# Channel shuffle: loads and stores in turn on one queue, with half tiles at both ends

## The chip, the cores and the metric

The kernel runs on one core of a Trainium2 chip. The core has several engines with instruction streams of their own: TensorE (PE), VectorE (DVE), ScalarE (ACT), GpSimd (POOL) and SyncE (SP). Data moves between the main memory (HBM) and the on-chip memory of 128 partitions by 16 DMA engines, which work from queues; a transfer is put on a queue by an instruction on one of the engine streams, here SyncE or ScalarE. In the profile "SPq" and "ACTq" are those issuing streams, and "q1" and "q10" their DMA queues.

The metric is the device time of one execution in microseconds, the median of several runs. Beside it there is one profiled execution with a trace.

## The reference

The input `x` has the shape 16 x 64 x 64 x 256, float32, 67.11 MB. The 256 channels are seen as 8 groups of 32, and the two are swapped:

```python
x = x.reshape(batch, h, w, groups, channels_per_group)
x = x.transpose(0, 1, 2, 4, 3)
x = x.reshape(batch, h, w, c)
```

Each of the 65,536 rows of 256 numbers is thus permuted within itself: channel g·32 + j goes to j·8 + g. No arithmetic is done. All 67.11 MB must be read and all 67.11 MB written.

## The kernel before

The 65,536 rows are cut into 8 tiles of 64 rows a partition (`_SLOTS = [[64]] * 8`). A tile is 128 partitions x 64 rows x 256 numbers, 64 KB a partition and 8.39 MB in all, contiguous in main memory. On chip it lives in a slot; three slots (`_BUFS = 3`) are used in rotation, each with room for 68 rows a partition.

Every tile goes through three steps.

1. Load (line 55): one transfer, issued by SyncE, puts the tile into its slot four rows after the slot's beginning (`_SHIFT = 4`).
2. Permute (line 64): 16 copies on VectorE, each of 4 rows a partition (1,024 numbers). A copy reads 4 rows and writes them, permuted, 4 rows earlier in the same slot. It writes where the copy before it has read, so no second buffer is needed, and the copies of a tile follow each other in order.
3. Store (line 68): one transfer, issued by ScalarE, of the 64 permuted rows that now stand at the beginning of the slot.

The order on each engine is the order in which the program is written (`manual_schedule`). Only the data and the slots make an engine wait: a copy waits for the tile's load, a store for the tile's 16 copies, and a load for the store of the tile that had the slot three tiles earlier. So loads 0, 1 and 2 are issued at once, and load k+3 waits on SyncE until store k has landed. Loads are on one queue and stores on another, and both queues may have work at the same time.

Of the kernel before, what the change touches and what calls it, by code (L numbers as in the profile page):

```python
# [1 line left out]

# [4 lines left out]


F32 = mybir.dt.float32
P = 128  # L10


_SLOTS = [[64]] * 8
_BUFS = 3

_SHIFT = 4


@with_exitstack
def kernel(  # L20
    ctx: ExitStack,
    tc: tile.TileContext,
    x: bass.AP,
    groups: bass.AP,
    out: bass.AP,
):
    nc = tc.nc
    b, h, w, c = x.shape
    G = int(groups)
    CPG = c // G  # L30
    assert G * CPG == c
    assert sum(map(sum, _SLOTS)) * P == b * h * w
    room = max(map(sum, _SLOTS)) + _SHIFT

    x_flat = x.rearrange("b h w c -> (b h w c)")
    out_flat = out.rearrange("b h w c -> (b h w c)")

    pool = ctx.enter_context(tc.tile_pool(name="pool", bufs=_BUFS))

    def rows(flat, first, q):  # L40

        return flat[first * c : (first + P * q) * c].rearrange("(p f) -> p f", p=P)

    ctx.enter_context(tc.manual_schedule(engines=None))
    first = 0
    for parts in _SLOTS:
        slot = pool.tile([P, room * c], F32, name="slot")
        at = 0
        pieces = []
        for q in parts:  # L50
            pieces.append((q, first, at))
            first += P * q
            at += q
        for q, start, at in pieces:
            nc.sync.dma_start(  # L55
                out=slot[:, (at + _SHIFT) * c : (at + _SHIFT + q) * c],
                in_=rows(x_flat, start, q),
            )
        for q, start, at in pieces:
            for lo in range(at, at + q, _SHIFT):  # L60
                n = min(_SHIFT, at + q - lo)
                src = slot[:, (lo + _SHIFT) * c : (lo + _SHIFT + n) * c]
                dst = slot[:, lo * c : (lo + n) * c]
                nc.vector.tensor_copy(  # L64
                    out=dst.rearrange("p (i j g) -> p i j g", j=CPG, g=G),
                    in_=src.rearrange("p (i g j) -> p i j g", g=G, j=CPG),
                )
            nc.scalar.dma_start(
                out=rows(out_flat, start, q), in_=slot[:, at * c : (at + q) * c]
            )  # L70


# [1 line left out]
_INS = ['x', 'groups']  # L74
_OUTS = [((16, 64, 64, 256), 'float32')]

_NUMBERS = {'groups': 8}


# [26 lines left out]
```

## Time and profile before

| | us |
|---|---|
| median of 3 runs | 322.84 (321.92 to 322.93) |
| the profiled execution | 322.83 |
| its span, first to last instruction | 321.1 |
| VectorE busy, 128 copies | 140.2 |
| a copy, mean | 1.095 |
| VectorE idle before a copy, for a load | 155.2, in 8 waits |
| SyncE waiting on line 55 for stores to land | 233.9, in 5 waits |
| issue to landing, loads (least, median, most) | 21.9, 44.1, 77.4 |
| issue to landing, stores (least, median, most) | 20.7, 55.7, 61.2 |

The profile counts the time that an engine spends in its instructions as busy; issuing a transfer is not counted. A transfer is listed with its issue and its landing. The DMA share is the mean busy share of the 16 DMA engines, and the GB/s are what they moved, reads of main memory and writes to it together. "Idle before, releaser" says what an instruction was waiting for when its engine stood still. In the chain of waits, each step is followed back to what released it. Some of its steps for this kernel are marked as released from "another core or an unknown queue"; they lie in the middle of the span, between one load's issue and the next.

### The profile page before, as it was taken

Reading aid. Unit: us, or ns where it says so; the run is one execution under the profiler, and the core shown is the slowest. Engines: PE = TensorE matmul, PEld = TensorE weight load, DVE = VectorE, ACT = ScalarE, POOL = GpSimd, SP = SyncE. Lnnn points to the kernel's source line nnn. Section 1 sums busy time; section 2 is a strip of 40 time slices with the busy share of each in tenths; the row PEclk is TensorE's granted clock in tenths of the full one; section 3 lists DMA queues with packets and bytes.
Section 4 is the critical chain, followed back from the end, with each engine's and each line's share of the span. In section 5 each row is a group of like instructions: output and inputs, shape, how many; then the busy total and the mean of one; then the engine's idle time right before and its main releaser. Section 6 shows DMA issues by size and latency. Waiting matters only on the chain.

```text
span 321.1 us, 207 instructions
## 1 busy us (share of the span) xinstructions
DVE 140.2 (44%) x128; POOL 0.2 (0%) x4
## 2 busy tenths in 40 slices
DVE  0019989401990006950069500795007940099300
POOL 0000000000000000000000000000000000000000
DMA  9999999999999999999999999999999999994696
GB/s 392 392 400 514 392 392 392 523 392 392 514 400 392 506 408 392 450 457 392 449 457 400 425 465 416 425 465 400 408 498 384 416 482 408 416 482 188 261 523 261
DMA packets 2305, 134.23 MB, mean 418 GB/s; under 512 B 256, under 2 KB 256, under 8 KB 256
## 3 DMA queue, kind: packets, MB, share of 16 engines
q1 hardware_dynamic: 1152, 67.11, 49.0%
q10 hardware_dynamic: 1152, 67.11, 48.3%
q14 instruction: 1, 0.01, 0.0%
HBM read 67.11 MB, written 67.11 MB: 418 GB/s over the span
## 4 chain that ended last, share of the span: by engine, by line
another core or an unknown queue 48%; DMA 33%; DVE 11%; SPq 0%; issue 0%; DVEq 0%
DMA slot<-in_x_dram 20%; DMA out_dram<-slot 13%; DVE slot L64 11%; SPq L55 0%; DVEq L64 0%
## 5 line engine op out<-in xcount | busy, mean ns | idle before, releaser
L64 DVE COPY slot<-slot 128x1024 f32<-128x1024 f32 x128 | 140.2, 1095 | 159.3 <-DMA slot<-in_x_dram 155.2
L87 POOL MEMSET const-bfloat16-1.0<- 128x1 bf16 x1 | 0.1, 101 | 0.0
L87 POOL MEMSET const-uint8-127<- 128x1 uint8 x1 | 0.1, 101 | 0.0
L87 POOL MEMSET const-float32-0.0<- 128x1 f32 x1 | 0.1, 98 | 0.2 <-issue 0.2
L87 POOL MEMSET const-float32-1.0<- 128x1 f32 x1 | 0.1, 98 | 0.0
## 6 DMA issues: line engine op xcount, KB each, us to landing
slot<-in_x_dram SPq DMA_DIRECT2D x8, 44.1
out_dram<-slot ACTq DMA_DIRECT2D x8, 55.7
```

The costliest lines, as they stand in the source:

```text
L64: nc.vector.tensor_copy(out=dst.rearrange("p (i j g) -> p i j g", j=CPG, g=G), in_=src.rearrange("p (i g j) -> p i j g", g=G, j=CPG),)
L87: nc = _bacc.Bacc("TRN2", target_bir_lowering=False, num_devices=1)
```

## The change

The slots stay three and of the same size. What changes:

- The tiles are nine: one of 32 rows a partition, seven of 64, one of 32 (`_TILES`). The first and the last are half as large, 4.19 MB and 8 copies each. The two half tiles move in transfers of 32 KB a partition.
- Stores are issued by SyncE, on the same queue as the loads. ScalarE issues nothing.
- The program is written so that SyncE's order is load 0, load 1, store 0, load 2, store 1, load 3, and so on to load 8, store 7, store 8: store k, and then load k+2.

The waits by data and by slots remain as they were. Load k+2 takes the slot of tile k-1, so it waits for the landing of store k-1; load 2 takes the third slot, which is free. On SyncE, what stands behind a waiting instruction waits with it: load k+2 cannot be issued before store k, and store k not before the copies of tile k. The copies themselves and their order on VectorE are the same, 128 in all.

```diff
-_SLOTS = [[64]] * 8
+_TILES = [32] + [64] * 7 + [32]
+_AHEAD = 2
 _BUFS = 3
...
+    queue = nc.sync
...
+    def load(k):
+        q = _TILES[k]
+        slots[k] = pool.tile([P, room * c], F32, name="slot")
+        queue.dma_start(
+            out=slots[k][:, _SHIFT * c : (_SHIFT + q) * c], in_=rows(x_flat, firsts[k], q)
+        )
+
+    def permute(k):
+        q, slot = _TILES[k], slots[k]
+        for lo in range(0, q, _SHIFT):
...
+            nc.vector.tensor_copy(
+                out=dst.rearrange("p (i j g) -> p i j g", j=CPG, g=G),
+                in_=src.rearrange("p (i g j) -> p i j g", g=G, j=CPG),
+            )
+
+    def store(k):
+        q = _TILES[k]
+        queue.dma_start(out=rows(out_flat, firsts[k], q), in_=slots.pop(k)[:, : q * c])
+
     ctx.enter_context(tc.manual_schedule(engines=None))
-    first = 0
-    for parts in _SLOTS:
...
-            nc.sync.dma_start(
...
-            nc.scalar.dma_start(
-                out=rows(out_flat, start, q), in_=slot[:, at * c : (at + q) * c]
-            )
+    n = len(_TILES)
+    for k in range(-_AHEAD, n):
+        if k >= 0:
+            permute(k)
+            store(k)
+        if k + _AHEAD < n:
+            load(k + _AHEAD)
```

More of the change, by code (lines that the diff above doesn't have):

```diff
@@ L31 @@
     assert G * CPG == c
-    assert sum(map(sum, _SLOTS)) * P == b * h * w
-    room = max(map(sum, _SLOTS)) + _SHIFT
+    assert sum(_TILES) * P == b * h * w
+    room = max(_TILES) + _SHIFT
     x_flat = x.rearrange("b h w c -> (b h w c)")
@@ L38 @@
     pool = ctx.enter_context(tc.tile_pool(name="pool", bufs=_BUFS))
+    queue = nc.sync
     def rows(flat, first, q):
         return flat[first * c : (first + P * q) * c].rearrange("(p f) -> p f", p=P)
-    ctx.enter_context(tc.manual_schedule(engines=None))
-    first = 0
-    for parts in _SLOTS:
[L47 to L54, printed above, removed]
-            nc.sync.dma_start(
-                out=slot[:, (at + _SHIFT) * c : (at + _SHIFT + q) * c],
-                in_=rows(x_flat, start, q),
-            )
[L59 to L68, printed above, removed]
-                out=rows(out_flat, start, q), in_=slot[:, at * c : (at + q) * c]
-            )
@@ new lines @@
+    firsts = [P * sum(_TILES[:k]) for k in range(len(_TILES))]
+    slots = {}
+    def load(k):
[7 more added lines that the diff above has]
+        for lo in range(0, q, _SHIFT):
+            n = min(_SHIFT, q - lo)
+            src = slot[:, (lo + _SHIFT) * c : (lo + _SHIFT + n) * c]
+            dst = slot[:, lo * c : (lo + n) * c]
+            nc.vector.tensor_copy(
+                out=dst.rearrange("p (i j g) -> p i j g", j=CPG, g=G),
+                in_=src.rearrange("p (i g j) -> p i j g", g=G, j=CPG),
+            )
```

## The prediction

> **What bounds the kernel now.** I first read the page's slices, to see which resource is full; then the stretches between the landings of the loads, for the rate in each; then the waits, the groups on one tile and the chain, for where the transfers stop.
>
> Page, part 2 (each digit is the busy share of one fortieth of the span, in tenths) and part 3:
>
> ```profile
> DVE  0019989401990006950069500795007940099300
> DMA  9999999999999999999999999999999999994696
> q1 hardware_dynamic: 1152, 67.11, 49.0%
> q10 hardware_dynamic: 1152, 67.11, 48.3%
> HBM read 67.11 MB, written 67.11 MB: 418 GB/s over the span
> ```
>
> The DMA engines are at nine tenths or more in 37 of the 40 slices, VectorE is busy 44% in bursts. So DMA bounds the kernel, and only two things can be had: the rate while it works, and the slices 36 and 37 (digits 4 and 6) near the end.
>
> Stretches cut at load landings (us, VectorE busy and instructions, POOL, PE clock, DMA share, GB/s):
>
> ```profile
> 22.60:41.90 19.30, 17.52 (x16) 0.00 (x0) 1.00 1.00 435
> 41.90:79.00 37.10, 17.50 (x16) 0.00 (x0) 1.00 1.00 424
> 79.00:117.70 38.70, 17.50 (x16) 0.00 (x0) 1.00 1.00 434
> 198.00:237.60 39.60, 17.62 (x16) 0.00 (x0) 1.00 0.99 425
> 281.40:299.50 18.10, 17.50 (x16) 0.00 (x0) 1.00 0.64 279
> 299.50:320.20 20.70, 0.00 (x0) 0.00 (x0) 1.00 0.94 405
> 41.90:281.40 239.50, 105.13 (x96) 0.00 (x0) 1.00 1.00 430
> ```
>
> Row 1 is load 1 alone, already queued behind load 0: 8.39 MB in 19.3 us, 435 GB/s. The last row is loads and stores mixed from two queues: 430. Row 5 is the hole: load 7 has landed, only the rest of store 6 is left, and store 7 cannot start until VectorE has done its 16 copies; the DMA engines work 64% of 18.1 us, 6.5 us lost. Row 6 is store 7 alone.
>
> The hole in the chain of work (start, us, what) and in the instructions in order of time:
>
> ```profile
> 237.61 43.75 DMA slot<-in_x_dram
> 281.36 0.03 issue
> 281.45 18.02 DVE L64 COPY slot<-slot 128x1024 f32<-128x1024 f32 x16 [20.74 <-DMA slot<-in_x_dram]
> 299.50 0.34 ACTq L68 DMA_DIRECT2D out_dram<-slot  x1
> ```
>
> Load 7 lasts 43.75 us because store traffic takes half of every engine beside it; then 18 us of copies, then 20.7 us of store, with nothing left to overlap.
>
> **The change part by part.** Every sum is made against the profiled execution: span 321.1 us, own time 322.83, so 1.73 us lie around the span; the median of the runs is 322.84, which is the same.
>
> *Bytes.* Unchanged. A 64-row transfer queued behind another takes the step between the landings of loads 0 and 1: 0.73 + 21.88 = 22.61 (the chain), and 41.94 (just before VectorE starts on it at 41.96), so 19.33 us. All bytes are 16 such transfers: 16 x 19.33 = 309.3 us.
>
> *Start and end.* The first load takes 21.88, so 2.55 us more than 19.33 (latency and first packets); it is issued at 0.73. From the last landing (320.2) to the span's end 0.9. So a queue that never runs dry ends at 0.73 + 2.55 + 309.3 + 0.9 = 313.5. This is 7.6 us under 321.1, about the 6.5 us hole plus the slower rate in the middle.
>
> *Does the one queue run dry?* SyncE issues load 0, load 1, store 0, load 2, store 1, load 3, ..., load 8, store 7, store 8. Store k waits for the 16 copies of tile k; load k+2 for the landing of store k-1, whose slot it takes. All issues now cost SyncE's time (0.33 us for a load, 0.34 for a store, 18 of them, 6 us in all) but beside the transfers. At the start: load 0 (32 rows) lands at 0.73 + 2.55 + 9.67 = 12.95, its 8 copies at 18.02/16 = 1.126 end at 22.0, and store 0 and load 2 (a free third slot, no wait) go out then; load 1 lands at 12.95 + 19.33 = 32.3. Cover 10.3 us. In the middle: when load k lands, the queue still holds store k-1 and load k+1, 38.7 us of work; store k is ready after 18.1 us. Behind it on SyncE waits load k+2, for store k-1, which lands 19.3 us plus a receipt after load k. Cover 20 us. At the end: when load 7 lands, store 6 and load 8 are left, 29.0 us, and its copies need 18.1; tile 8's copies start when load 8 lands and end 9.0 us later under store 7 (19.3 us). Store 8 is then already queued. So the hole goes, and nothing is late next. If VectorE needed over 29 us for a tile the last cover would be gone.
>
> *ScalarE's queue* loses its 8 store issues, which stood beside everything: nothing. *Two transfers more* (18 for 16), with packets of half the size in four: the completion entries of the 16 DMA engines are the only extra work; loads 0 and 1 back to back, such an entry between them, ran at 435 GB/s. Nothing to 0.1 us each; I take nothing.
>
> *Interleaving.* Loads and stores no longer share an engine packet by packet; they come in blocks, 8 changes from load to store and 7 back. No row shows two directions following on one queue. Lower bound nothing: in the mixed rows every engine changes direction from packet to packet, and 79.0 to 117.7, where store 0 also ends and store 1 follows on its queue, ran at 434. Upper bound from the rows near to it: at the one place where an all-load stretch first meets a store (43 to 47 us), the packet records of the trace show one packet on each of the 16 engines at 2.9 to 3.5 us where the others take 2.42, on average 0.8 us. Changes back to loads show none. I take this 0.8 once, where the first store comes, and nothing later, since the steady rows are nearest in kind; the ends are 0 and 8 x 0.85 = 6.8.
>
> *Engines out of step.* The packet records show the 16 engines ending loads 0 to 3 within 0.7 us of each other, but store 6 between 293.3 and 297.7. Today the hole absorbs this; in a queue that is full to the end the slowest engine sets the end. Ends 0 and 4.4; I take 1.5, nearer to the low end, because the drift grew only in the mixed stretch of two queues.
>
> Sum: 313.5 + 0.8 + 1.5 = 315.8, and with 1.73 around it 317.5 us.
>
> *A rule against it.* The row first: the step of 19.33 us between queued transfers leaves no room for a fixed cost per transfer. The Trainium skill, "DMA: Bandwidth & Descriptors", section "Anatomy of one DMA — SWDGE (gpsimd) path", gives every DMA about 2.0 us that do not scale with its size, most of it waiting for the write's receipt, fitted on another issue path than the one here. An estimate by that page alone, with all 18 transfers strictly one after another, is 134.22 MB at 436 GB/s plus 36 us, 344 us; the row says the cost is paid at the ends only.
>
> **The rivals.**
>
> *B, the other side: a bubble at each change of direction.* One ring does what two did, so while a store waits for its last writes no other ring fills the engine. Full price from the isolated transfers: a store alone 20.66 - 19.33 = 1.33, a load alone 2.55; 8 x 1.33 + 7 x 2.55 = 28.5, from 313.5 + 1.5 + 1.73 = 316.7 to 345. It decides from 0.47 us a change over 15 changes (316.7 + 7.1 = 323.8). At 0.85 on the 8 changes to stores only, 323.5: no change. For it: the slow packets at 43 us, and no row of one queue with both directions. Against it: the completion of load 0 cost its queue nothing, nor did that of store 0 (434 GB/s around it).
>
> *C, the engines drift as now.* The slowest is 4.4 us late: 313.5 + 0.8 + 4.4 + 1.73 = 320.4. With the whole middle at today's 430 GB/s, 134.22 / 0.430 = 312.1 for 309.3, it is 318.0. For it: rows at 424 and 425. Against: the pure load row at 435.
>
> *D, the change does not do what it says: the queue still runs dry.* A store waits for VectorE longer than the work queued, and a hole like today's stays: 317.5 + 6.5 = 324. Against it the covers of 10, 20 and 11 us; VectorE's 1.1 us a copy hardly varies.
>
> **How the numbers follow.** The likeliest 0.72, its own range 314.2 to 318.8: no drift and no first change give 315.2, a first load with packets half as long may save up to 1 us of the start, and drift 2.5 with a second slow change gives 319. C 0.13. B 0.13, of which 0.05 within the bound of 0.3% (321.9 to 323.8, what a measurement of this kernel can tell from no change) and 0.08 above. D 0.02. Faster 0.85, same 0.05, slower 0.10. The range runs from 314.2 through C into the lower part of B, to 322.5; about 0.14 is left out.
>
> **What would show it.** Right: a DMA line of nines to the last slice; 434 or 435 GB/s in every stretch from 12 us on; load landings about 38.7 us apart in the middle; SyncE's waits for stores long but VectorE's start on each tile at once after its load; last landing at 312 to 315. Wrong in the changes: a load or store in the queue that takes 20 us or more, with the DMA share down at each boundary and 410 to 425 GB/s throughout. Wrong in the covers: a DMA digit under 9 in mid-span with SyncE waiting for VectorE. The forecast fails if blocks of one direction are slower than packets in turn, which no row of this profile shows.

## The result and the profile after

The changed kernel takes 319.56 us (median of 6 runs, 318.73 to 319.86) where the kernel before takes 322.88 beside it (6 runs, 321.31 to 325.28). The ratio is 0.9886, with a 95% interval of 0.9841 to 0.9931: faster by 1.1%, about 3.3 us where 5.3 were forecast, and 2.1 us above the forecast of 317.5. Ratios here and below are taken over undisturbed runs, so one can differ a little from the ratio of the two medians. The profiled execution took 319.86 us with a span of 318.1.

The page of the changed kernel, parts 2 and 3:

```profile
DVE  0370794199101990029900299003980049707300
DMA  8999999999999999999999999999999999899984
q1 hardware_dynamic: 2592, 134.22, 98.5%
HBM read 67.11 MB, written 67.11 MB: 422 GB/s over the span
```

The hole of before (digits 4 and 6, slices 37 and 38 of the 40; the prediction counts them from zero) is gone, and one queue carries everything. What is left is an 8 in the first slice, an 8 in slice 35, and the end with 8 and 4.

Stretches of the changed kernel, cut at load landings and around the last copies (us, VectorE, POOL, PE clock, DMA share, GB/s):

```profile
62.80:102.00 39.20, 17.52 (x17) 0.00 (x0) 1.00 0.99 428
102.00:141.10 39.10, 17.49 (x16) 0.00 (x0) 1.00 1.00 429
141.10:180.50 39.40, 17.53 (x17) 0.00 (x0) 1.00 1.00 428
258.80:288.30 29.50, 17.48 (x16) 0.00 (x0) 1.00 1.00 429
288.30:297.30 9.00, 8.74 (x8) 0.00 (x0) 1.00 1.01 437
297.30:317.20 19.90, 0.03 (x1) 0.00 (x0) 1.00 0.80 346
62.80:258.80 196.00, 87.52 (x80) 0.00 (x0) 1.00 1.00 431
```

While VectorE works on the last tile (288.3 to 297.3) the DMA engines now run at 437 GB/s; before they ran at 279 beside the last copies. But the middle runs at 431 and not at 434 or 435, and a load and a store together take 39.1 to 39.4 us where two transfers of 19.33 would take 38.66. The last stretch has a share of 0.80. Some engines are finished before others there: by the packet records (the trace's list of single DMA packets) they end between 313.6 and 316.9 us.

The instructions in order of time, with the waits:

```profile
62.78 18.01 DVE L62 COPY slot<-slot 128x1024 f32<-128x1024 f32 x16 [11.44 <-DMA slot<-in_x_dram]
80.82 0.34 SPq L69 DMA_DIRECT2D out_dram<-slot  x1
82.35 0.33 SPq L52 DMA_DIRECT2D slot<-in_x_dram  x1
101.96 18.05 DVE L62 COPY slot<-slot 128x1024 f32<-128x1024 f32 x16 [21.17 <-DMA slot<-in_x_dram]
```

Store 2 goes out at 80.82, as soon as its tile is permuted, and load 4 at 82.35, when store 1 has landed. Load 3, already in the queue, lands only at 101.9. The queue held work for 20 us, as forecast.

### The profile page after: what moved, and what is told of

Its sections match the earlier page's. It is cut to its first block, busy times and chain, and to the rows that moved or that the text cites. A ratio compares the mean times of both kernels' runs of the same rounds, so it can differ in the third digit from the quotient of the medians.

```text
span 318.1 us, 206 instructions
## 1 busy us (share of the span) xinstructions
DVE 140.0 (44%) x128; POOL 0.2 (0%) x4
## 4 chain that ended last, share of the span: by engine, by line
DMA 45%; DVE 27%; another core or an unknown queue 20%; issue 1%; SPq 0%; DVEq 0%
DMA slot<-in_x_dram 32%; DVE slot L62 27%; DMA out_dram<-slot 13%; SPq L69 0%; DVEq L62 0%
```

## The experiments

Times are medians; each ratio is to the kernel before, run on the same chip beside it. The prediction's base of 313.5 us is the span of a queue that is never empty.

**1. The two parts apart.** The tiles alone: the stores go back to ScalarE's queue.

```diff
     queue = nc.sync
+    store_queue = nc.scalar
...
-        queue.dma_start(out=rows(out_flat, firsts[k], q), in_=slots.pop(k)[:, : q * c])
+        store_queue.dma_start(out=rows(out_flat, firsts[k], q), in_=slots.pop(k)[:, : q * c])
```

> The nine tiles of the changed kernel, with the stores back on ScalarE's queue: the tile sizes alone. When the last half tile has landed, store 7 is still to run, so VectorE's 9 us are covered and the hole of 6.5 us should be gone here too. Theory A (the gain is the hole, whoever closes it): 313.5 + 2.8 for the middle at 430 GB/s + 1 to 3 for the engines out of step + 1.7 around the span, 319 to 321, about the time of the changed kernel. Rival (the queue itself gives the gain): within 1 us of 322.9.

Measured: 319.15 us, ratio 0.9918 (0.9887 to 0.9948), as theory A has it. While VectorE works on the last tile the DMA engines are full:

```profile
292.40:301.40 9.00, 8.76 (x8) 0.00 (x0) 1.00 1.06 459
```

The one queue alone:

```diff
-_TILES = [32] + [64] * 7 + [32]
+_TILES = [64] * 8
```

> The one queue in turn, with eight tiles of 64 rows: the order of the queue alone. Load 7 is followed by store 6, 19.3 us, and the copies of tile 7 need 18.1, so store 7 is issued about 1 us before the queue is empty. Theory A: the half tiles add nothing to the one queue, 319 to 320.5 as with them, 8 changes from load to store as there. Rival (the half tiles carry the gain): a hole at the end as before, 322 to 325.

Measured: 320.90 us, ratio 0.9954 (0.9931 to 0.9976), between theory A and the rival. The stretches of this kernel after load 7 has landed:

```profile
279.00:297.10 18.10, 17.48 (x16) 0.00 (x0) 1.00 0.88 380
297.10:317.80 20.70, 0.01 (x1) 0.00 (x0) 1.00 0.94 405
```

Store 6 stands beside the last copies, and of the hole (0.64 and 279 GB/s before) a small one is left (0.88 and 380). The cover of about 1 us that was expected does not suffice: 15 of the 16 engines end store 6 between 295.4 and 297.2 us, store 7 is issued at 297.14, and its first packets start at 298.0. They stand still for 1.7 us on the mean of the 16. The tiles alone give 0.8%, the one queue alone 0.5% and both together 1.1%, with an interval that overlaps that of the tiles alone. The gains do not add up, since both parts close the same hole.

**2. What the missing 2 us are.** In the packet records of the changed kernel, a load's last packet is longer than the others where a store follows it on the queue: on all 16 engines by 0.6 to 1.6 us before store 0, on 7 to 16 of them by some 0.1 to 0.8 before stores 1 to 6, on none before store 7. On the mean of the engines this is 1.0 us at store 0 and 1.5 at all later stores together. Packets at a change back to loads are not longer. If each change from load to store has a price, kernels with more and fewer changes show it. Twice as many:

```diff
-_TILES = [32] + [64] * 7 + [32]
+_TILES = [32] * 16
```

> The one queue in turn with sixteen tiles of 32 rows: 16 changes from load to store for 8, and 32 transfers for 18. Theory C (each change from load to store costs every engine about 0.3 us, the first 1.0, and puts the engines further apart): 8 changes cost 318.1 - 313.5 = 4.6 us of span, 0.57 each, so 8 more give 319.6 + 4.6 = about 324, with a slow last packet in every load. Rival T (the engines fall out of step with time or bytes, whatever the order): 319 to 320.

Measured: 323.57 us, ratio 1.0039 (1.0017 to 1.0061). The time is that of theory C, but mostly not for its reason, as the page and the copies of tiles 7, 13 and 15 (the last) show:

```profile
DMA  8979999999999999999999999999999999999957
```

```profile
144.83 9.04 DVE L62 COPY slot<-slot 128x1024 f32<-128x1024 f32 x8 [11.21 <-DMA slot<-in_x_dram]
262.84 9.04 DVE L62 COPY slot<-slot 128x1024 f32<-128x1024 f32 x8 [11.17 <-DMA slot<-in_x_dram]
301.65 8.99 DVE L62 COPY slot<-slot 128x1024 f32<-128x1024 f32 x8 [10.32 <-DMA slot<-in_x_dram]
```

The queue runs empty at both ends. Load 1 has ended on every engine by 22.5 us, and store 0, issued at 22.21, starts its packets at 23.05: 1.2 us of standing still on the mean. At the end 9.67 us of store 14 must cover 9.0 us of copies. The engines end it between 306.0 and 310.9 us, the last store is issued at 310.67 and starts at 311.5: 4.0 us on the mean. Longer packets take only 0.9 us more than in the changed kernel, for 8 more changes. Between 144.83 and 262.84 VectorE starts 6 tiles further, 19.67 us each; two queued transfers of 9.67 are 19.33, so 0.34 us too much for each change. About half of that (0.17) is on the mean of the engines; the rest is that the slowest falls further behind the mean, from 2.0 to 3.4 us. Twice as many again, `_TILES = [16] * 32`:

> The one queue in turn with thirty-two tiles of 16 rows: 32 changes from load to store. From 8 to 16 changes the time rose 4.0 us, 0.50 each. Theory C, if the price is the same for each: 323.6 + 16 x 0.50 = 331.6. Rival (tiles of 32 were slower for the half-size packets or for the empty queue at their start, not for the changes): packets of 16 KB at the same rate, 323 to 326.

Measured: 333.31 us, ratio 1.0299 (1.0234 to 1.0365): 9.7 us for 16 more changes. The queue runs empty at both ends here too, by about as much. By the packet records, longer packets account for 6.5 us of the difference, 0.4 for each change, and the packets of 16 KB, 0.611 us each where half of a 32 KB packet's 1.213 is 0.607, for some 2. So neither run gives the price by its time alone. The run that parts changes from transfers is this one, with four slots of 44 rows in place of three of 64:

```diff
-_TILES = [32] + [64] * 7 + [32]
-_AHEAD = 2
-_BUFS = 3
+_TILES = [44] * 8 + [40] * 4
+_BATCH = 4
+_BUFS = 4
...
-    for k in range(-_AHEAD, n):
-        if k >= 0:
+    for b in range(0, n, _BATCH):
+        for k in range(b, min(b + _BATCH, n)):
+            load(k)
+        for k in range(b, min(b + _BATCH, n)):
             permute(k)
             store(k)
-        if k + _AHEAD < n:
-            load(k + _AHEAD)
```

> One queue, twelve tiles of 44 and 40 rows in four slots, in the order of four loads, then four stores: 3 changes from load to store in place of 8, 24 transfers for 18. Theory C (a price for each change): 313.5 + 1.0 + 2 x 0.3 + 1 to 1.5 for engines out of step + 1.7, 317.8 to 318.3, 1.3 to 1.8 faster than the changed kernel. Rival T (time or bytes): 319.6 as the changed kernel. Rival N (a price for each transfer): 319.6 + 6 x 0.25 = 321.

Measured: 317.66 us, ratio 0.9852 (0.9827 to 0.9878). Here are 24 transfers where the changed kernel has 18, but 3 changes where it has 8, and it is faster. In neither does an engine stand still for long, so the ends do not disturb this comparison. To compare the two directly, both were run again on one chip:

> The changed kernel, beside the batches of four on the same chip: 319 to 320. It stands here for the difference to the next run.

> Twelve tiles in batches of four loads and four stores on one queue, 3 changes from load to store. Theory C (a price for each change): 1.5 to 2.5 under the changed kernel, 317 to 318. If the lead in the run before was the spread between chips and calls: within 0.7 of the changed kernel.

Measured: 318.83 (318.61 to 319.69) and 317.37 (317.17 to 318.42), six runs each that do not overlap: 1.5 us, ratios 0.9876 and 0.9831 to the kernel before. A cycle of four loads and four stores in the first run of the batches, from the landing of load 3 to that of load 7:

```profile
57.50:164.90 107.40, 48.23 (x45) 0.00 (x0) 1.00 1.00 432
```

Eight transfers of 44 rows at 19.33 x 44/64 = 13.29 are 106.3 us; the cycle has 1.1 us more. By the packet records only about 0.3 of it is on the mean of the engines, with the one change; 0.7 is that the slowest engine falls further behind the mean, from 0.34 to 1.08 us. The changed kernel pays about 0.55 in each 39 us: 0.23 on the mean, 0.33 by the slowest engine. The longer packets before stores come to 1.0 us in the whole run of the batches (0.87, 0.11 and 0.04 at its three changes) and to 2.5 in the changed kernel. The other limit is a kernel with a single change. It leaves out seven of the eight stores, so that most of the output is not written, and moves the same bytes, 125.83 MB of loads and 8.39 MB of store:

```diff
-_TILES = [32] + [64] * 7 + [32]
+_TILES = [64] * 8
+_PASSES = [0, 1, 2, 3, 4, 5, 6, 7, 0, 1, 2, 3, 4, 5, 6]
+_STORED = 12
...
+    for i, k in enumerate(_PASSES):
+        load(k)
+        if i == _STORED + 2:
+            queue.dma_start(out=rows(out_flat, firsts[kept[0]], _TILES[kept[0]]), in_=kept[1][:, : _TILES[kept[0]] * c])
+        permute(k)
+        if i == _STORED:
+            kept = (k, slots[k])
```

> The same 134.22 MB on one queue, but fifteen loads of 64 rows (tiles 0 to 7 and again 0 to 6, all copied on VectorE) and one store, of tile 4 alone: the other seven stores are left out, so most of the output isn't written. One change from load to store. Theory C: 313.5 + 1.0 + at most 0.7 for engines out of step + 1.7 = 315.2 to 317. Rival T (the engines fall out of step with time or bytes): 313.5 + 1.0 + 3 + 1.7 = 319.

Measured: 317.36 us (317.20 to 317.47), span 315.6; 0.4 above the upper end of theory C and 1.6 below the rival. Its first copies (the view ends at 62 us):

```profile
22.71 18.06 DVE L64 COPY slot<-slot 128x1024 f32<-128x1024 f32 x16 [22.71 <-DMA slot<-in_x_dram]
42.04 18.11 DVE L64 COPY slot<-slot 128x1024 f32<-128x1024 f32 x16 [1.27 <-DMA slot<-in_x_dram]
61.38 1.08 DVE L64 COPY slot<-slot 128x1024 f32<-128x1024 f32 x1 [1.23 <-DMA slot<-in_x_dram]
```

Without changes the first landings are 19.33 us apart, with VectorE busy nearly all the time. In the packet records 15 of the 16 engines end within 0.44 us of each other and one 1.9 us after the middle one, which it became mostly in two steps, at 80 to 84 and at 236 to 240 us. The last packet before the one store, at 293 us, is not longer on any engine: this change shows no price. So both things are there, longer packets before some stores and a loss on single engines that comes without changes, but the price is not the same for each change, and theory C's 1.0 us for the first one is not seen here. What makes the packet before a store longer, and why here it does not, was not tested and stays open.

**3. Is one queue needed for the batches?** The batches of four with the stores on ScalarE, by the same edit as in the first experiment.

> The batches of four with the stores on ScalarE's queue: nothing then holds a store back behind the loads, so store 0 goes out at 29 us beside load 2, and the engines turn packet by packet again. Theory C with a price only for blocks that change on one queue: no slow packets but at the first store, the middle at 430 GB/s as in the kernel before, 318.5 to 320. Rival Q (what counts is how few transfers wait, not the queue): 317 to 318 as on one queue.

Measured: 319.09 us, ratio 0.9863 (0.9815 to 0.9911). The six times fell into two groups, two at 317.0 and four at 319.1 to 319.7, and the profile is of the second. In that profile 12 of the 16 engines stand still before the last store, 1.9 us on the mean of the 16. It decides nothing between the two expectations.

**4. Is it only the last tile?** One line of the kernel before, in its own order and with its own two queues:

```diff
-_SLOTS = [[64]] * 8
+_SLOTS = [[64]] * 7 + [[32]] * 2
```

> The kernel before with one line changed: seven tiles of 64 rows and two of 32, two queues, its own order. Theory A (the hole of the last tile is all the gain): the last tile's copies take 9 us with store 7 half as long beside them, the hole shrinks from 6.5 us to 0 to 2; 318.5 to 320.5, as the changed kernel. Rival (the half tile at the front or the order on SyncE is needed): 321.5 or more.

Measured: 324.33 us, ratio 1.0024 (0.9984 to 1.0064): no gain. Theory A as I had worked it out fails here, and the profile says where. The chain of work and then the stretches of this kernel:

```profile
222.34 43.24 DMA out_dram<-slot
...
265.65 35.85 DMA slot<-in_x_dram
```

```profile
273.10:282.50 9.40, 8.75 (x8) 0.00 (x0) 1.00 0.93 390
282.50:301.60 19.10, 0.01 (x1) 0.00 (x0) 1.00 0.99 412
301.60:310.60 9.00, 8.75 (x8) 0.00 (x0) 1.00 0.27 117
310.60:321.60 11.00, 0.00 (x0) 0.00 (x0) 1.00 0.89 381
```

The last load moves half as much as load 7 of the kernel before, and takes 35.85 us where an equal share of the engines would give 19.3. When it lands the stores beside it are nearly done, and 9 us of copies stand at 117 GB/s. The hole has only moved. In the nine tiles of the first experiment the last half load took as long (issued at 254.98, copies from 292.40), but the store before the last is of 64 rows there, and still ran beside the last copies; here it is of 32. The reason for the slow load would be that the engines give the two queues one packet in turn, whatever its size: 32 KB of load for 64 KB of store. The load then gets a third of an engine, 29.0 us; by the packet records the engines end it 29.0 to 35.5 us after its issue. Two kernels test that, again by one line of the kernel before:

```diff
-_SLOTS = [[64]] * 8
+_SLOTS = [[64]] * 7 + [[32, 32]]
```

> The kernel before with the last tile in two pieces of 32 rows in one slot: two loads, copies, two stores. Theory S (the engines give one packet to each queue in turn, so a load in packets of 32 KB gets a third of the engine beside stores in packets of 64): the loads of the pieces take 16 x (1.21 + 2.42) = 58 us from 237.6, the second lands at about 296 and not at 281.4 as before; a store of 32 rows stands beside its 9 us of copies, so no hole, 318 to 320. Rival (both queues get the same share of bytes): the second piece lands at 281 to 284.

Measured: 324.42 us, ratio 1.0067 (1.0037 to 1.0098), slower than before. Its last stretches:

```profile
284.00:304.90 20.90, 2.15 (x2) 0.00 (x0) 1.00 0.96 386
304.90:313.90 9.00, 6.66 (x7) 0.00 (x0) 1.00 0.41 175
```

The second piece was issued at about 235.9 and its copies began at 302.72, 66.8 us later: later even than the 58 us of two thirds for the stores, and far from the 281 to 284 of equal shares. In the packet records load and store packets follow each other in turn for the most part, and the engines end the second piece 59.5 to 66.4 us after its issue, so what goes beyond 58 is in the main that they are out of step. The expected 318 to 320 was missed, since with the load that late the stores beside it had run out. Then the same cut for all tiles, so that all packets are equal:

```diff
-_SLOTS = [[64]] * 8
+_SLOTS = [[32, 32]] * 8
```

> The kernel before with every tile in two pieces of 32 rows in one slot: all packets are 32 KB. Theory S: equal packets share equally again, the last piece lands at 279 to 285 as in the kernel before; the hole is 9 us of copies with store 7a and the rest of store 6 beside them, so closed, 318 to 320. Rival (small pieces cost in themselves, a price for each of the 32 transfers): 322 or more.

Measured: 317.01 us (316.88 to 317.26), ratio 0.9828 (0.9789 to 0.9867). The page of this kernel, the copies of its last two pieces, and its stretches:

```profile
DMA  8999999999999999999999999999999999999996
```

```profile
273.31 8.96 DVE L64 COPY slot<-slot 128x1024 f32<-128x1024 f32 x8 [10.29 <-DMA slot<-in_x_dram]
292.67 9.01 DVE L64 COPY slot<-slot 128x1024 f32<-128x1024 f32 x8 [10.40 <-DMA slot<-in_x_dram]
```

```profile
41.90:275.00 233.10, 105.37 (x97) 0.00 (x0) 1.00 1.00 434
285.00:295.00 10.00, 2.26 (x3) 0.00 (x0) 1.00 0.99 426
295.00:305.00 10.00, 6.51 (x6) 0.00 (x0) 1.00 1.03 446
```

Pieces land 19.3 us apart to the end, a 9.67 us load beside an equal store: equal packets share equally. The time of the last landing was forecast too early (279 to 285; it is 292.6), because the pieces start their stores earlier, so loads and stores share from 26 us on. The time is 1 us below the 318 to 320 expected. The hole is closed (446 GB/s beside the last copies), and the middle runs at 434 GB/s, the rate that the changed kernel did not reach. This is the fastest kernel of the study, with the order and the two queues of before; the batches of four on one queue (0.9831) are level with it.

The Trainium skill, "DMA: Bandwidth & Descriptors", section "Queues, rings and completion order", says that a DMA engine takes turns between the queues that have work, a packet at a time. The runs agree, a packet in their records being the 32 or 64 KB of one partition: with half packets against whole ones the half-size load needs 35.85 us, with equal packets two pieces follow at 19.3.

## Why the prediction was right, and where it was off

*What bounds the kernel, and the hole.* Right. The bytes set the time, and the hole beside the last copies went from 279 GB/s to 437. The tiles alone close it, the one queue alone closes most of it. Closing it did not give its whole price: by the packet records the engines stand still 6.2 us less than before on the mean, but longer packets take 0.9 us back, and the slowest engine, 0.1 us behind the mean at the end before, is 2.2 behind now.

*The covers* (10, 20 and 11 us). Right: store 0 went out at 21.98 (22.0 forecast) while load 1 landed at 33.3 (32.3), the middle stores 20 us ahead, and store 8 was issued at 297.4 while store 7 ran. Rival D fell for this kernel. Where the cover was 1 us or less it came true: 1.7 us of standing still with eight tiles of 64 on one queue, 4.0 before the last store with sixteen of 32.

*Bytes, start and end,* 313.5. Right. Load 0 landed at 12.95 as forecast, and in the kernel with a single change the first queued loads landed 19.33 apart.

*Interleaving,* priced at 0.8 once and nothing later. This is the step that failed: it held that "the steady rows are nearest in kind". Steady turns by packet between two queues do not tell what blocks in one queue cost. By the packet records, the mean of the engines ended at 314.65 us where load 0's mean end, 12.33, and 15.5 transfers of 19.33 give 311.9: 2.7 us, and not 0.8. Of these, 2.5 are the longer packets before stores, 1.0 before store 0, near the 0.8 forecast, and 1.5 at the later stores, for which nothing was taken. Rival B named the right place with too high a price: 2.7 us in all, where 7.1 would have decided, so the kernel stayed faster. Its empty engine is not in the records: what they show is a longer packet, and no engine stands still for over 0.4 us between two. Sixteen changes do not decide for it either, since that kernel's 323.57 us hold 5.2 us of standing still at the two ends.

*Engines out of step,* 1.5. The slowest engine ended 2.2 us after the mean, 0.3 of which was there at load 0, so 1.9 (in the second profile 1.4 after the mean); mis-sized a little. The reason given for the low end, that the drift grew only where two queues were mixed, does not hold: in the kernel with a single change, loads alone on one queue, the slowest engine went from 0.4 to 1.8 us behind the mean. Rival C's 320.4 is nearer to the 319.56 than the likeliest case's 317.5, but not by its own cause, which was 4.4 us of drift; its second figure, 318.0, leaves out the 0.8 and any drift.

The sum then reads 313.5 + 2.7 + 1.9 = 318.1, the measured span, where 0.8 and 1.5 had given 315.8.

*The two further transfers and the fixed cost.* With 64 transfers on one queue (tiles of 16) the time is 333.31 us. By the 2.0 us that the Trainium skill, "DMA: Bandwidth & Descriptors", section "Anatomy of one DMA — SWDGE (gpsimd) path", gives each DMA, an estimate for 64 strictly one after another is 308 + 128 = 436 us. No run shows that for queued transfers.

*The signs named ahead.* The nines came, but with slices at 8 and a last one of 4; the rate of the middle was 431 and not 434; landings were 39.2 and not 38.7 apart; the last landing was at 317.2 and not at 312 to 315. The time lies in the range given, above the likeliest case's own range; that the range reached it is owed to rivals B and C, not to the likeliest case.

## What to carry to other kernels

Where transfers bound a kernel, look for the stretch in which nothing is left to move beside the last computation, and close it; which edit does that matters less than that it is closed, and two that do so do not add up. On one queue fewer changes of direction went with less time here (3 against 8: 317.4 and 318.8 us); on two queues look at the packet sizes, since a transfer in small packets gets less than its share beside one in large packets. Making only the last tile smaller can starve just the transfer on which the end waits. A cover of 1 us or less is none: issue, start and the slowest engine used it up here.

## What was not expected

- On one queue a load's last packet can be longer where a store follows. In the changed kernel this is 1.0 us on the mean of the engines at the first change, 0.15 to 0.33 at the next six and nothing at the eighth; in the batches 0.9, 0.1 and 0.0; at the single change at 293 us nothing. A change back to loads shows it too, with eight tiles of 64 (store 0's last packet before load 2, 0.5 to 1.2 us longer on all engines). With 3 and 8 changes the times were 317.4 to 317.7 and 318.8 to 319.6 us; the 323.6 and 333.3 us with 16 and 32 also hold the empty queue at both ends.
- On two queues in the order of before, half-size packets did worst in the last tile only (324.3 and 324.4 us) and best where all were of that size (317.0 us). In the latter the loads and stores stay in step: the 16 engines end each load and each store within 1.9 us of each other, while before they ended store 6 up to 4.4 us apart.
- The tiles alone with two queues took 319.15 us and the tiles with one queue 318.8 to 319.6: moving the stores to SyncE's queue in itself neither gave nor cost a measurable time.
